# Reading the moving columns of every projection in two interleaved runs, with two moves in the first projection, in a four-layer transformer kernel

## The chip, the cores and the metric

One Trainium2 chip, one of its NeuronCores. The metric is device time in microseconds from the start to the end of one execution. TensorE (PE) multiplies, VectorE (DVE) and ScalarE (ACT) work on elements, GpSimd (POOL) on a few small rows, SyncE (SP) issues most of the DMAs.

## What is computed

Two small transformers of two layers each run one after the other on 256 tokens with 1024 features, all in float32. Layer by layer:

```python
x = x + fox_mixer(rms_norm(x, g))       # 16 heads, causal softmax with a forget gate
x = x + square(relu(rms_norm(x, g) @ w_up)) @ w_down
x = x + mla_mixer(rms_norm(x, g))       # 8 heads, low-rank q, shared low-rank k and v
x = x + square(relu(rms_norm(x, g) @ w_up)) @ w_down
x = rms_norm(x, g)
x = x + gla_mixer(rmsnorm(x, g))        # 4 heads, gated linear attention in chunks of 64
x = x + (silu(conv(h @ w_a)) * conv(h @ w_u)) @ w_down
x = x + (b * conv(c * u)) @ w_out       # b, c, u = rmsnorm(x, g) @ w_in
x = x + (silu(conv(h @ w_a)) * conv(h @ w_u)) @ w_down
return rmsnorm(x, g)
```

The work is nearly all in the projections `h @ w` with weights of 1024 rows and up to 5632 columns.

## The kernel before

**Split operands.** A float32 product is made of three matmuls of type fp32r. Each weight and each activation is kept as a high part and a low part: `wh` is the weight rounded to fp32r (a cast on ACT, line 294, or 291 with a gain), `wl` is the rest (a subtraction on DVE, line 312, or 308), and `hh` and `hl` are the same for the normalized activations. `mm3` issues `hh*wh`, `hh*wl` and `hl*wh` into one PSUM tile. Line 339 is the only line that issues these matmuls, so the profile gives them all under L339, told apart by their tiles: a name such as `up<-hh,wh` is the output tile, the moving operand and the stationary one.

**Two kinds of projection.** `proj`, `proj_wide` and `accum` keep 128 tokens stationary and move 512 (or 264, 320, 384) weight columns; their output has tokens on the partitions. `proj_T` keeps 128 weight columns stationary and moves the 256 tokens; its output is transposed, and two such outputs of 256 columns lie side by side in a PSUM tile of 512. Attention, the chunks of the linear attention and the transposes use plain float32 operands that are not split, with the same `mm` or with `transpose`.

**Evacuation.** When a PSUM tile is complete, a callback reads it: `by_row` on DVE (lines 399 and 401, times a row of scales), `add_x` on DVE (579 and 581, onto the residual), `scaled` on ACT (591, times a column of scales), a Relu on ACT (616), and a few more. `scaled_wide` cuts the two halves of a 528-column output into 512 columns of v and 16 of a gate.

**Weights.** SP loads raw weights into four buffers; `pump` casts the next units ahead (five buffers each of `wh` and `wl`), `pump_lo` makes their low parts.

**Order.** Most of the order comes from the program itself: `after(n, f)` runs `f` after `n` ticks, and a tick is one group of three matmuls (or six); the table `DLY` holds the delays. The engines run in program order, so what one waits for holds up all that comes behind it. The beginning, `start`, is written out by hand in a manual schedule: transposes of the four blocks of `x`, gains, the high and low parts of each block (`high(t, c)` and `low(t, c)` for token half t and feature half c), and the first weight splits between them. `norm` gathers the sums of squares; its last `stat` sets the scales on POOL and, where a row of them is wanted (`row`), calls `make_row` after `DLY[35]` ticks, which is 1: a DVE copy (line 144), two transposes on PE (line 502), an ACT copy (line 148). The row's readers are the `by_row` calls.

Of the kernel before, what the change touches and what calls it, by code (L numbers as in the profile page):

```python
# [15 lines left out]
ALU = mybir.AluOpType  # L16
# [144 lines left out]
class Builder:  # L161
# [178 lines left out]

    def mm3(self, ps, h, u, kk, n, start, stop):
# [18 lines left out]
    def proj(self, h, nk, n, evac, tiles=None, k0=0):  # L360
# [3 lines left out]
        while k < nk:  # L364
            u = self.unit()
            for kk in range(u.kn):
                for t in range(2):
                    self.mm3(ps[t][:, :n], h.get(t, k), u, kk, n, k == 0, k == nk - 1)
                    if k == nk - 1:
                        evac(t, ps[t])  # L370
                    self.tick()
                k += 1

    def proj_T(self, h, nk, evac, tile_fn=None):
# [4 lines left out]
        while k < nk:  # L379
            u = self.unit()  # L380
            for kk in range(u.kn):
                hh, hl = h.both(k)
                for f in range(4):
                    o = ps[f // 2][:, f % 2 * S:f % 2 * S + S]
                    wh, wl = [x[:, kk, f * P:(f + 1) * P] for x in (u.hi, u.lo)]
                    self.mm(o, wh, hh, k == 0 and f % 2 == 0, False)
                    self.mm(o, wl, hh, False, False)
                    self.mm(o, wh, hl, False, k == nk - 1)
                    if f % 2:
                        if k == nk - 1:  # L390
                            evac(f // 2, ps[f // 2])
# [3 lines left out]
    def by_row(self, out, ps, row, mul=None):  # L395

        r = lambda x: x.rearrange("p (i s) -> p i s", i=2)
        if mul is None:
            self.nc.vector.tensor_tensor(out=r(out), in0=r(ps), in1=row, op=ALU.mult)
        else:  # L400
            self.nc.vector.scalar_tensor_tensor(out=r(out), in0=r(ps), scalar=mul, in1=row, op0=ALU.mult, op1=ALU.mult)  # L401

    def proj_wide(self, h, evac, tile_fn):
# [3 lines left out]
        for k in range(8):  # L407
            if k % 2 == 0:
                u = self.unit()
            for t in range(2):  # L410
                hh, hl = h.get(t, k)
                for i in range(2):
                    o = ps[t][i][:, :n]
                    wh, wl = [x[:, k % 2, i * n:i * n + n] for x in (u.hi, u.lo)]
                    self.mm(o, hh, wh, k == 0, False)
                    self.mm(o, hh, wl, False, False)
                    self.mm(o, hl, wh, False, k == 7)
                if k == 7:
                    evac(t, *ps[t])
                self.tick()  # L420

    def scaled_wide(self, out, a, b, col):

        n = WIDE // 2
        self.scaled(out[:, 0:n], a[:, 0:n], col)
        self.scaled(out[:, n:512], b[:, 0:512 - n], col)
        return b[:, 512 - n:n]

    def accum(self, acc, h, ks, first, last, done=None, cs=(0, 1)):

        for c in cs:
            k = 0
            while k < len(ks):
                u = self.unit()
                for kk in range(u.kn):
                    for t in range(2):
                        self.mm3(acc[t][c], h.get(t, ks[k]), u, kk, 512, first and k == 0, last and k == len(ks) - 1)
                        if last and k == len(ks) - 1:
                            done(t, c, acc[t][c])
# [3 lines left out]
    def accum_by_token(self, acc, h, ks, done):  # L443
# [4 lines left out]
        self.nc.vector.tensor_tensor(out=xs, in0=acc[1][1], in1=xs, op=ALU.add)  # L448
        for t in range(2):
            for c in range(2):  # L450
                if not (t and c):
# [3 lines left out]
                    done(t, c, acc[t][c], 0)  # L455
                    continue
                for o in (0, 256):
                    ps = self.up_tile()[:, 0:256]
                    for i, k in enumerate(ks):
                        hh, hl = h.get(t, k)  # L460
                        wh, wl = [x[:, i, o:o + 256] for x in (us[c].hi, us[c].lo)]
                        self.mm(ps, hh, wh, i == 0, False)
                        self.mm(ps, hh, wl, False, False)
                        self.mm(ps, hl, wh, False, i == n - 1)
                        self.tick()
                    done(t, c, ps, o)
# [77 lines left out]
    def norm(self, gains, square=False, row=None, tile_fn=None, early=0):  # L544
# [7 lines left out]
        def stat(t, c):  # L552
            self.square_sum(ss[:, 2 * c + t:2 * c + t + 1], self.x[t][c], 512, 1.0 / 32.0)
            seen.append(1)
            if len(seen) == 4:
# [6 lines left out]
                if row is not None:  # L562
                    self.after(DLY[35], lambda: out.make_row(row))
# [9 lines left out]
    def add_x(self, hook, scale=None):  # L573
        nc = self.nc

        def done(t, c, ps, o=None):
            xs = self.x[t][c] if o is None else self.x[t][c][:, o:o + ps.shape[1]]
            if scale is None:
                nc.vector.tensor_tensor(out=xs, in0=ps, in1=xs, op=ALU.add)
            else:  # L580
                nc.vector.scalar_tensor_tensor(out=xs, in0=ps, scalar=scale[:, t:t + 1], in1=xs, op0=ALU.mult, op1=ALU.add)
# [7 lines left out]
    def scaled(self, out, ps, col):  # L589

        self.nc.scalar.activation(out=out, in_=ps, func=AF.Copy, scale=col)
# [15 lines left out]
    def ffn1(self, h, rs, hook):  # L607
# [360 lines left out]
    def mla(self, h, rs, hook):  # L968
# [21 lines left out]
        def ev_kv(t, ps):  # L990
            c = self.tmp_tile()
            self.scaled(c[:, :256], ps[:, :256], rs[:, t:t + 1])
            self.scaled(kc[:, t * 64:(t + 1) * 64], ps[:, 256:320], rs[:, t:t + 1])
# [28 lines left out]
        def ev_q(t, ps):  # L1022
            c = self.tmp_tile()
            self.scaled(c[:, :384], ps[:, :384], rs[:, t:t + 1])
# [101 lines left out]
    def gla(self, h, rs, hook):  # L1126
# [93 lines left out]
        def ev_g(i):  # L1220
            def f(t, ps):
                gs = self.tmp_tile()
                nc.scalar.activation(out=gs, in_=ps, func=AF.Silu, scale=rs[:, t:t + 1])
# [198 lines left out]
    def sc(self, h, rs, hook):  # L1422
# [9 lines left out]
        def ev_u(i):  # L1432
            def f(b, ps):
                z = cs.pop(b)
                nc.vector.tensor_tensor(out=z, in0=ps, in1=z, op=ALU.mult)
# [8 lines left out]
        def ev_b(i):  # L1444
            def f(b, ps):
                c = cv.pop(b)
                nc.vector.tensor_tensor(out=c, in0=ps, in1=c, op=ALU.mult)
# [280 lines left out]
```

## Time and profile before

| | before |
|---|---|
| median of 3 runs | 1157.27 us (1157.15 to 1157.37) |
| the profiled execution | 1156.24 us |
| its span | 1154.5 us |
| PE busy | 1142.0 us (99%) |
| PE weight loads busy (beside matmuls) | 1030.1 us (89%) |
| DVE busy | 804.8 us (70%) |
| ACT busy | 610.9 us (53%) |
| matmuls recorded | 7769 |
| DMA moved | 207.30 MB, mean 180 GB/s |

A matmul's own duration in the profile reaches from its start to its modelled end and overlaps the next one's; the time that a row of matmuls takes is their distance from start to start. The table gives averages over stages; the rows below give single stretches.

### The profile page before, as it was taken

Reading aid. Unit: us, or ns where it says so; the run is one execution under the profiler, and the core shown is the slowest. Engines: PE = TensorE matmul, PEld = TensorE weight load, DVE = VectorE, ACT = ScalarE, POOL = GpSimd, SP = SyncE. Lnnn points to the kernel's source line nnn. Section 1 sums busy time; section 2 is a strip of 40 time slices with the busy share of each in tenths; the row PEclk is TensorE's granted clock in tenths of the full one; section 3 lists DMA queues with packets and bytes.
Section 4 is the critical chain, followed back from the end, with each engine's and each line's share of the span. In section 5 each row is a group of like instructions: output and inputs, shape, how many; then the busy total and the mean of one; then the engine's idle time right before and its main releaser. Section 6 shows DMA issues by size and latency. Waiting matters only on the chain.

```text
span 1154.5 us, 19192 instructions
## 1 busy us (share of the span) xinstructions
PE 1142.0 (99%) x7769; PEld 1030.1 (89%) x7769; DVE 804.8 (70%) x1196; ACT 610.9 (53%) x923; POOL 33.2 (3%) x55
## 2 busy tenths in 40 slices
PE   8999999999999999999999999999999999999997
PEld 6987998998888999899898789999989999999996
DVE  6686755555686755555788569777786668887775
ACT  5465554445665545444563556455555446555453
POOL 0000100000000100000010000000001000000001
PEclk9999999999999999999999999999999999999999
DMA  9744455555463556555555355556665564656551
GB/s 341 276 146 146 160 197 191 183 183 167 135 203 120 168 192 195 192 184 183 185 178 170 110 165 164 180 179 191 200 217 185 194 185 134 196 175 213 183 159 62
DMA packets 137802, 207.30 MB, mean 180 GB/s; under 512 B 10529, under 2 KB 65009, under 8 KB 137713
## 3 DMA queue, kind: packets, MB, share of 16 engines
q1 hardware_dynamic: 136576, 203.89, 55.1%
q10 hardware_dynamic: 1136, 2.17, 0.5%
q8 instruction: 61, 1.00, 0.4%
q14 instruction: 29, 0.23, 0.1%
HBM read 204.97 MB, written 1.07 MB: 178 GB/s over the span
## 4 chain that ended last, share of the span: by engine, by line
PE 92%; DVE 5%; ACT 2%; issue 1%; POOL 0%; ACTq 0%; DVEq 0%; POOLq 0%
PE up L339 52%; PE acc L339 37%; DVE wl L312 1%; PE acc L502 1%; ACT p L672 1%; DVE p L691 1%; PE tp L502 1%; ACT wh L294 0%; DVE p L682 0%; ACT junk L535 0%; PE tp L512 0%; DVE kT L1207 0%; PE acc L1582 0%; DVE pT L700 0%; DVE bias L758 0%
## 5 line engine op out<-in xcount | busy, mean ns | idle before, releaser
L312 DVE TENSOR_TENSOR wl<-raw,wh 128x1024 fp32r<-128x1024 f32 (+2 forms) x373 | 454.1, 1219 | 261.4 <-ACT wh L294 259.5
L294 ACT CAST wh<-raw 128x1024 fp32r<-128x1024 f32 (+2 forms) x373 | 389.5, 1045 | 432.3 <-PE up L339 278.2
L339 PE MATMUL up<-hh,wh 128*128 128x256 f32 x1564 | 439.2, 281 | 0.0
L339 PE MATMUL up<-hh,wl 128*128 128x256 f32 x1564 | 437.7, 280 | 0.0
L339 PE MATMUL up<-hl,wh 128*128 128x256 f32 x1564 | 436.5, 280 | 0.0
L339 PEld LDWEIGHTS up<-hh,wh 128*128 128x128 f32 x1564 | 294.3, 188 | 3.0 <-issue 1.5
L339 PEld LDWEIGHTS up<-hh,wl 128*128 128x128 f32 x1564 | 294.1, 188 | 1.5
L339 PEld LDWEIGHTS up<-hl,wh 128*128 128x128 f32 x1564 | 294.2, 188 | 0.3 <-DVE hl L491 0.2
L339 PE MATMUL acc<-wh,hh 128*128 128x512 f32 (+1 forms) x606 | 235.8, 389 | 0.2 <-DVE mx L691 0.2
L339 PE MATMUL acc<-wh,hl 128*128 128x512 f32 (+1 forms) x606 | 233.3, 385 | 0.0
L339 PE MATMUL acc<-wl,hh 128*128 128x512 f32 (+1 forms) x606 | 232.8, 384 | 0.0
L339 PEld LDWEIGHTS acc<-wh,hl 128*128 128x128 f32 x606 | 113.8, 188 | 24.5 <-DVE hl L708 0.3
L339 PEld LDWEIGHTS acc<-wh,hh 128*128 128x128 f32 x606 | 113.8, 188 | 23.1 <-DVE mx L691 0.6
L339 PEld LDWEIGHTS acc<-wl,hh 128*128 128x128 f32 x606 | 113.9, 188 | 21.6
L1340 DVE SCALAR_TENSOR_TENSOR tmp<-tmp,vecs,tmp 128x255 f32<-128x255 f32 x192 | 78.0, 479 | 18.0 <-ACT tmp L1338 18.0
L339 PE MATMUL up<-wh,hh 128*128 128x512 f32 (+4 forms) x142 | 53.9, 382 | 0.3 <-DVE tmp L401 0.3
L339 PE MATMUL up<-wl,hh 128*128 128x512 f32 (+4 forms) x142 | 51.6, 364 | 1.3 <-DVE wl L312 1.3
L339 PE MATMUL up<-wh,hl 128*128 128x512 f32 (+4 forms) x142 | 51.4, 364 | 0.0
L1338 ACT ACTIVATE tmp<-tmp,vecs 128x256 f32<-128x256 f32 x96 | 40.9, 497 | 0.0
L1349 DVE TENSOR_TENSOR hl<-tmp,hh 128x512 fp32r<-128x512 f32 x58 | 38.2, 685 | 0.0
L1348 ACT CAST hh<-tmp 128x512 fp32r<-128x512 f32 x58 | 34.2, 622 | 2.2 <-DVE tmp L1393 2.2
L339 PEld LDWEIGHTS up<-wh,hh 128*128 128x128 f32 x142 | 26.7, 188 | 7.5 <-issue 3.4
(205 smaller groups left out, 770.5 us busy)
## 6 DMA issues: line engine op xcount, KB each, us to landing
raw<-ffn_w_up SPq DMA_DIRECT2D x176, 256.0 KB, 4.1
raw<-ffn_w_up SPq DMA_DIRECT2D x32, 1024.0 KB, 5.4
raw<-ffn_w_down SPq DMA_DIRECT2D x32, 1024.0 KB, 5.0
raw<-ffn_w_down SPq DMA_DIRECT2D x44, 512.0 KB, 6.5
raw<-sc_w_in SPq DMA_DIRECT2D x12, 1024.0 KB, 5.2
raw<-fox_w_in SPq DMA_DIRECT2D x10, 1024.0 KB, 9.4
raw<-gla_w_in SPq DMA_DIRECT2D x10, 1024.0 KB, 5.1
raw<-fox_w_out SPq DMA_DIRECT2D x4, 1024.0 KB, 5.0
```

Source lines behind the costliest of these rows:

```text
L294: self.last_hi = nc.scalar.copy(hi[:, :kn, :w], self.raws[r][:, k:k + kn])
L312: self.last_wl = nc.vector.tensor_tensor(out=u.lo[:, :kn, :w], in0=self.raws[r][:, k:k + kn], in1=u.hi[:, :kn, :w].bitcast(F32), op=ALU.su ...
L339: self.nc.tensor.matmul(out, lhsT, rhs, start=start, stop=stop, skip_group_check=True)
L502: self.nc.tensor.transpose(tp[:, i * P:(i + 1) * P], src[:, i * P:(i + 1) * P], self.ident)
L672: self.nc.scalar.activation(out=p[:, o:o + n], in_=p[:, o:o + n], func=AF.Exp, scale=scale, bias=nm[:, j:j + 1], accum_out=sm[:, j:j + 1])
L691: self.nc.vector.tensor_tensor_reduce(out=p[:, o:o + n], in0=lgs[h][:, w], in1=bias(h)[:, w], scale=1.0, scalar=NEG, op0=ALU.add, op1=ALU. ...
L1338: nc.scalar.activation(out=out, in_=z, func=AF.Copy, scale=w[:, 2:3])
L1340: nc.vector.scalar_tensor_tensor(out=out[:, d:], in0=z[:, :S - d], scalar=w[:, 2 - d:3 - d], in1=out[:, d:], op0=ALU.mult, op1=ALU.add)
L1348: nc.scalar.copy(hi, src)
L1349: nc.vector.tensor_tensor(out=lo, in0=src, in1=hi.bitcast(F32), op=ALU.subtract)
```

## The change

Every matmul of the split projections now goes through `mmw`. It hands the moving operand over as two runs, the first and the second half of its columns, taken in turn: column 0, column n/2, column 1, column n/2 + 1 and so on. The output is written in consecutive order, so PSUM holds the columns woven. Whoever reads PSUM undoes this by a view (`woven`) that takes every second column, and `like` gives the other operands the same shape. Where an instruction cannot take so many dimensions, it is cut in two (`by_row` with a factor, `scaled_wide`); the evacuation of the 320 columns of the shared k and v now copies all 320 in one piece, and the 64 rotary columns again.

In the first projection the low part of the second weight unit is made ahead of the last activation block's low part (`pump_lo(2)` before `low(1, 1)`), and the first layer's row of scales is made 12 ticks after the scales are set, not 1 (`row_at`). Other rows keep 1.

The diff, cut to its core:

```diff
+    def mmw(self, out, lhsT, rhs, start, stop):
+        self.mm(out.rearrange("p (b a) -> p b a", a=2), lhsT, rhs.rearrange("p (a b) -> p b a", a=2), start, stop)
+
+    @staticmethod
+    def woven(ps, n=1):
+        return ps.rearrange("p (b a) -> p a b", a=2) if n == 1 else ps.rearrange("p (i b a) -> p i a b", i=n, a=2)
...
     def mm3(self, ps, h, u, kk, n, start, stop):
         hh, hl = h
         wh, wl = u.hi[:, kk, :n], u.lo[:, kk, :n]
-        self.mm(ps, hh, wh, start, False)
-        self.mm(ps, hh, wl, False, False)
-        self.mm(ps, hl, wh, False, stop)
+        self.mmw(ps, hh, wh, start, False)
+        self.mmw(ps, hh, wl, False, False)
+        self.mmw(ps, hl, wh, False, stop)
...
     def by_row(self, out, ps, row, mul=None):
-        r = lambda x: x.rearrange("p (i s) -> p i s", i=2)
+        out, row = self.like(out, ps), self.like(row, ps)
         if mul is None:
-            self.nc.vector.tensor_tensor(out=r(out), in0=r(ps), in1=row, op=ALU.mult)
+            self.nc.vector.tensor_tensor(out=out, in0=ps, in1=row, op=ALU.mult)
         else:
-            self.nc.vector.scalar_tensor_tensor(out=r(out), in0=r(ps), scalar=mul, in1=row, op0=ALU.mult, op1=ALU.mult)
+            for i in range(2):
+                self.nc.vector.scalar_tensor_tensor(out=out[:, i], in0=ps[:, i], scalar=mul, in1=row[:, i], op0=ALU.mult, op1=ALU.mult)
...
     def scaled_wide(self, out, a, b, col):
         n = WIDE // 2
-        self.scaled(out[:, 0:n], a[:, 0:n], col)
-        self.scaled(out[:, n:512], b[:, 0:512 - n], col)
-        return b[:, 512 - n:n]
+        m = n // 2
+        self.scaled(out[:, 0:n], a, col)
+        self.scaled(out[:, n:n + m], b[:, 0], col)
+        self.scaled(out[:, n + m:512], b[:, 1, :m - 16], col)
+        return b[:, 1, m - 16:]
...
-                    self.after(DLY[35], lambda: out.make_row(row))
+                    self.after(row_at, lambda: out.make_row(row))
...
             def f(b, ps):
                 r = self.tmp_tile()
-                nc.scalar.activation(out=r, in_=ps, func=AF.Relu)
+                nc.scalar.activation(out=self.like(r, ps), in_=ps, func=AF.Relu)
...
             stat(1, 1)
             low(0, 1)
+            self.pump_lo(2)
             low(1, 1)
-            self.pump_lo(2)
...
-        hook, rs = self.norm([(h, self.vec("mix0"))], row=0)
+        hook, rs = self.norm([(h, self.vec("mix0"))], row=0, row_at=12)
```

The reading order itself does not show in a list of instructions, since a matmul's size stays the same. The two moves do. On DVE, in `start` and the beginning of the first layer (`hl_182` is the low part of the second feature half's activations, `wl_187` of the second weight unit, `rs_117` the scales; lines from 1543 on are 25 higher in the change):

```order
L1568 TENSOR_TENSOR hl_182<-tmp_174,hh_181 128x4x128
L1568 TENSOR_TENSOR hl_182<-tmp_184,hh_181 128x4x128
L312 TENSOR_TENSOR wl_187<-raw_106,wh_186 128x2x512
L312 TENSOR_TENSOR wl_229<-raw_106,wh_228 128x2x512
L144 COPY tmp_212<-rs_117 128x256
L312 TENSOR_TENSOR wl_240<-raw_231,wh_239 128x1056
L312 TENSOR_TENSOR wl_246<-raw_231,wh_245 128x1056
L312 TENSOR_TENSOR wl_250<-raw_234,wh_249 128x1056
```

and in the change:

```order
L1593 TENSOR_TENSOR hl_182<-tmp_174,hh_181 128x4x128
L312 TENSOR_TENSOR wl_187<-raw_106,wh_186 128x2x512
L1593 TENSOR_TENSOR hl_182<-tmp_184,hh_181 128x4x128
L312 TENSOR_TENSOR wl_222<-raw_106,wh_221 128x2x512
L312 TENSOR_TENSOR wl_233<-raw_224,wh_232 128x1056
L312 TENSOR_TENSOR wl_239<-raw_224,wh_238 128x1056
L312 TENSOR_TENSOR wl_243<-raw_227,wh_242 128x1056
L144 COPY tmp_280<-rs_117 128x256
```

The second weight unit's low part has moved ahead of the second `hl_182`, and the copy of the scales behind three splits of the wide projection. On PE, the matmuls that read them (the transposes of line 502 are 21 lines further down in the change), before:

```order
L339 MATMUL up_119<-wh_186,hh_181 128x512
L339 MATMUL up_118<-wl_187,hh_181 128x512
L339 MATMUL up_118<-wh_186,hl_182 128x512
L339 MATMUL up_119<-wl_187,hh_181 128x512
L339 MATMUL up_119<-wh_186,hl_182 128x512
L339 MATMUL up_118<-wh_186,hh_181 128x512
L339 MATMUL up_118<-wl_187,hh_181 128x512
L502 MATMUL tp_214<-ident,tmp_212 128x128 x2
L339 MATMUL up_118<-wh_186,hl_182 128x512
```

and, where the two transposes now stand:

```order
L339 MATMUL acc_299<-wh_232,hh_147 128x264
L339 MATMUL acc_299<-wl_233,hh_147 128x264
L523 MATMUL tp_282<-ident,tmp_280 128x128 x2
L339 MATMUL acc_299<-wh_232,hl_148 128x264
L339 MATMUL acc_296<-wh_232,hh_147 128x264
```

They have moved past the rest of the first projection, 16 matmuls, and the first 11 of the wide one.

## Rows read from the trace of the kernel before

**Rows 1.** The page, busy us, share of the span and instructions of each engine

```profile
PE   1142.0 (99%) x7769; PEld 1030.1 (89%) x7769; DVE 804.8 (70%) x1196; ACT 610.9 (53%) x923; POOL 33.2 (3%) x55
```

**Rows 2.** The page, chain that ended last: share of the span by engine, by line

```profile
PE 92%; DVE 5%; ACT 2%; issue 1%; POOL 0%; ACTq 0%; DVEq 0%; POOLq 0%
PE up L339 52%; PE acc L339 37%; DVE wl L312 1%; PE acc L502 1%; ACT p L672 1%; DVE p L691 1%; PE tp L502 1%; ACT wh L294 0%; DVE p L682 0%; ACT junk L535 0%; PE tp L512 0%; DVE kT L1207 0%; PE acc L1582 0%; DVE pT L700 0%; DVE bias L758 0%
```

**Rows 3.** The chain in order of time: start us, us, what, merged matmuls

```profile
24.37 9.98 PE acc L339 x82
...
147.58 11.09 PE acc L339 x48
158.66 11.22 PE up L339 x96
...
248.01 11.35 PE up L339 x96
...
721.90 11.28 PE up L339 x96
```

**Rows 4.** Timeline of PE, linear attention: start us, us, what, merged

```profile
634.85 1.89 PE L339 MATMUL acc<-v,both 128*128 128x256 f32 x8
```

**Rows 5.** PE's groups by shape: line, what, count, busy us, mean ns, idle

```profile
L339 PE MATMUL up<-hh,wh 128*128 128x256 f32 x1564 | 439.2, 281 | 0.0
...
L339 PE MATMUL acc<-wh,hh 128*128 128x512 f32 x558 | 222.1, 398 | 0.2 <-DVE mx L691 0.2
...
L339 PE MATMUL up<-wh,hh 128*128 128x512 f32 x90 | 37.4, 419 | 0.3 <-DVE tmp L401 0.3
...
L339 PE MATMUL acc<-wh,hh 128*128 128x264 f32 x48 | 13.7, 286 | 0.0
...
L339 PE MATMUL acc<-hh,wh 128*128 128x256 f32 x44 | 12.3, 280 | 0.0
...
L339 PE MATMUL up<-wh,hh 128*128 128x264 f32 x16 | 4.6, 290 | 0.0
...
L339 PE MATMUL acc<-v,both 128*128 128x256 f32 x16 | 3.8, 379 | 0.0
```

**Rows 6.** Timeline of PE, first projection: start us, us, what, idle before

```profile
13.03 0.63 PE L339 MATMUL up<-wh,hh 128*128 128x512 f32 x2
14.96 0.50 PE L339 MATMUL up<-wl,hh 128*128 128x512 f32 x1 [1.31 <-DVE wl L312]
...
17.56 0.44 PE L502 MATMUL tp<-ident,tmp 128*128 128x128 f32 x2 [0.94 <-DVE tmp L144]
```

**Rows 7.** Timeline of DVE and of ACT in the same stretch

```profile
13.08 0.69 DVE L1568 TENSOR_TENSOR hl<-tmp,hh 128x512 fp32r<-128x512 f32 x1 [0.78 <-ACT hh L1564]
13.69 2.35 DVE L312 TENSOR_TENSOR wl<-raw,wh 128x1024 fp32r<-128x1024 f32 x2
17.21 0.29 DVE L144 COPY tmp<-rs 128x256 f32<-128x256 f32 x1 [1.17 <-POOL rs L542]
17.42 4.76 DVE L312 TENSOR_TENSOR wl<-raw,wh 128x1056 fp32r<-128x1056 f32 x4
...
11.48 1.04 ACT L294 CAST wh<-raw 128x1024 fp32r<-128x1024 f32 x1
```

**Rows 8.** Stretches: length, busy us of PE, PEld, DVE, ACT, POOL, clock, DMA

```profile
53.00:97.00 44.00, 43.80 (x367) 35.43 (x366) 38.47 (x135) 26.75 (x76) 0.18 (x1) 1.00 0.53 184
...
125.00:300.00 175.00, 175.00 (x1139) 159.08 (x1138) 100.70 (x105) 85.16 (x105) 3.63 (x4) 1.00 0.55 180
...
593.00:619.00 26.00, 26.00 (x209) 25.20 (x207) 25.40 (x37) 16.66 (x21) 0.00 (x0) 1.00 0.49 160
...
676.00:863.00 187.00, 187.00 (x1339) 175.36 (x1338) 147.65 (x212) 104.23 (x146) 2.75 (x3) 1.00 0.59 183
```

**Rows 9.** Line 399's instructions: count, ns min/median/max, first and last start us

```profile
L399 DVE TENSOR_TENSOR tmp<-up,rowb x48: 680/684/692, 693.4 to 1129.9; 128x512 f32<-128x512 f32 x48
L399 DVE TENSOR_TENSOR kT<-up,rowb x8: 662/681/684, 46.9 to 346.4; 128x512 f32<-128x512 f32 x8
```

More of the change, by code (lines that the diff above doesn't have):

```diff
@@ L447, in accum_by_token @@
         xs = self.x[1][1]
-        self.nc.vector.tensor_tensor(out=xs, in0=acc[1][1], in1=xs, op=ALU.add)
+        ps = self.woven(acc[1][1])
+        self.nc.vector.tensor_tensor(out=self.like(xs, ps), in0=ps, in1=self.like(xs, ps), op=ALU.add)
         for t in range(2):
@@ L542, in rsqrt, with norm @@
         nc.gpsimd.tensor_tensor(out=out, in0=out, in1=self.mhalf[:, :n], op=ALU.pow)
-    def norm(self, gains, square=False, row=None, tile_fn=None, early=0):
+    def norm(self, gains, square=False, row=None, tile_fn=None, early=0, row_at=1):
         ss = self.small.tile([P, 4], F32, tag="ss", name=self.name("ss"))
@@ L576, in done @@
         def done(t, c, ps, o=None):
-            xs = self.x[t][c] if o is None else self.x[t][c][:, o:o + ps.shape[1]]
+            xs = self.x[t][c] if o is None else self.x[t][c][:, o:o + ps.shape[1] * ps.shape[2]]
+            x3 = self.like(xs, ps)
             if scale is None:
-                nc.vector.tensor_tensor(out=xs, in0=ps, in1=xs, op=ALU.add)
+                nc.vector.tensor_tensor(out=x3, in0=ps, in1=x3, op=ALU.add)
             else:
-                nc.vector.scalar_tensor_tensor(out=xs, in0=ps, scalar=scale[:, t:t + 1], in1=xs, op0=ALU.mult, op1=ALU.add)
+                nc.vector.scalar_tensor_tensor(out=x3, in0=ps, scalar=scale[:, t:t + 1], in1=x3, op0=ALU.mult, op1=ALU.add)
             if o is None:
@@ L589, in scaled @@
     def scaled(self, out, ps, col):
+        if len(ps.shape) > 2:
+            out = self.like(out, ps)
         self.nc.scalar.activation(out=out, in_=ps, func=AF.Copy, scale=col)
@@ L1222, in f @@
                 gs = self.tmp_tile()
-                nc.scalar.activation(out=gs, in_=ps, func=AF.Silu, scale=rs[:, t:t + 1])
+                nc.scalar.activation(out=self.like(gs, ps), in_=ps, func=AF.Silu, scale=rs[:, t:t + 1])
                 def gain():
@@ L1434, in f @@
                 z = cs.pop(b)
-                nc.vector.tensor_tensor(out=z, in0=ps, in1=z, op=ALU.mult)
+                nc.vector.tensor_tensor(out=self.like(z, ps), in0=ps, in1=self.like(z, ps), op=ALU.mult)
                 def go():
@@ L1446, in f @@
                 c = cv.pop(b)
-                nc.vector.tensor_tensor(out=c, in0=ps, in1=c, op=ALU.mult)
+                nc.vector.tensor_tensor(out=self.like(c, ps), in0=ps, in1=self.like(c, ps), op=ALU.mult)
                 self.after(DLY[29], lambda: self.split_pair(c, y, 4 * i + 2 * b))
```

43 lines of the change are left out of this document (24 added, 19 removed).

## The prediction

> **What bounds the kernel now.** I read the page first. TensorE (PE) is busy for 1142.0 of 1154.5 us, VectorE (DVE) for 70% of the span [rows 1], and the granted clock is 1.00 in the stretches that I looked at, the 2.4 GHz level [rows 8]. The chain of waits agrees: 92% of the end is set by PE, and 52% and 37% by the two kinds of matmul that line 339 issues [rows 2]. None of the lines that empty PSUM (399, 401, 579, 581, 591, 616) is among those that the chain names. So the time is the number of matmuls times their pitch (start to start), and the next question is what the pitch is made of.
>
> The chain in order of time gives pitches, since it merges a run of back-to-back matmuls into one piece [rows 3]: 48 matmuls with 512 moving columns in 11.09 us are 231.0 ns each; 96 with 256 columns take 11.22 to 11.35 us, 116.9 to 118.2 ns, and I use 117.3; 82 with 264 columns take 9.98 us, 121.7 ns. At one column a cycle of 2.4 GHz, 512 columns need 213.3 ns and 256 need 106.7. So 17.7 ns and 10.6 ns are lost, and the loss grows with the columns.
>
> Is that loss in the engine or in the supply of columns? The kernel holds a control. Its attention matmuls are plain fp32, not split: 8 of them with 256 columns take 1.89 us [rows 4], of which the last one's own 0.379 [rows 5] is not pitch, so (1.89 - 0.379) / 7 = 215.9 ns. That is two cycles a column (213.3 ns) and 2.5 ns more. A stream that asks for a column every second cycle loses only a fixed 2.5 ns; one that asks every cycle loses four to seven times as much. Contention with other engines does not look like the cause: the 256-column pitch is 11.22 to 11.35 us for 96 where DVE is busy for 100.7 of 175 us, and 11.28 [rows 3] where it is busy for 147.7 of 187 us [rows 8]. What is left is the way in which one run of consecutive fp32 columns is fetched, and that is what the change alters.
>
> **The change, part by part.** *The reading order.* The counts are in rows 5: (1564 + 44) x 3 = 4824 matmuls with 256 columns, (558 + 90) x 3 = 1944 with 512, (48 + 16) x 3 = 192 with 264. (The few with 320 and 384 columns I leave out.) They write PSUM in consecutive order as before, and no matmul is added. No row of the trace shows a moving operand read in two interleaved runs, so its price has to be bounded. The lower end: one cycle a column and the fixed 2.5 ns of the plain matmuls, which gives 109.2, 215.8 and 112.5 ns. The upper end: two cycles a column, as the plain ones, 215.9, 429.2 and 222.5 ns. I take the lower end: two streams half a tile apart give each stream the two cycles a column at which the plain matmuls show no loss, so the row nearest to what each stream now asks is the plain one, halved. The sum is 4824 x 8.1 ns = 39.1 us, 1944 x 15.2 ns = 29.5 us, 192 x 9.2 ns = 1.8 us: 70.4 us.
>
> The row speaks for this, a rule speaks against it. The Trainium skill (Advanced Engine Details and Errata, section Memory Cachelines) says that SBUF has 16-byte lines and that at least two hits in a row on one line are needed to absorb its latency; here neighbours lie 512 bytes or more apart, so no two reads in a row would meet one line. By that rule the order would be slower, not faster; no run here shows it yet. By the rows the sum is near 1091 us, by the rule it is that of the second rival below.
>
> *Where the gain does not arrive.* In two stages the chain runs through DVE and ACT rather than PE: 53 to 97 us (DVE busy for 38.5 of 44) and 593 to 619 us (25.4 of 26) [rows 8]. A faster PE waits there. At the average rate, 70.4 / 1142 = 6.2%, these 70 us would have given 4.3 us; I take off all of it, and 66.1 us stay. Elsewhere DVE has room: in 676 to 863 us it is busy for 147.7 us and PE would still need some 175.
>
> *The evacuations.* PSUM columns now lie woven, so DVE and ACT read every second one. No row shows a strided read. The lower bound is nothing: a read of 512 columns from PSUM takes 684 ns [rows 9], and one from SBUF 0.69 us [rows 7], so these reads are paced by the element. The upper bound is a doubling; since no such line reaches the list of the chain, whose last entries round to 0% (under 0.5%, 5.8 us) [rows 2], I put it at 6 us. I take 2 us, nearer to the rows. The split calls (two halves where a scalar factor is used, two pieces where the wide projection's tail is cut off) are eight or so more instructions on DVE and ACT, hidden beside PE; without that cover each would cost a few tenths of a microsecond.
>
> *The weight split ahead of the low part.* PE waits 1.31 us at 14.96 us for the low part of a weight [rows 6], which DVE makes at 13.69 us behind an hl that itself waited for ACT [rows 7]. Its input, the cast that starts at 11.48 and takes 1.04 us, is there at 12.52 [rows 7]. Placed ahead, the split runs from 12.52 to 13.74 us, and PE is ready at 13.03 + 2 x 0.231 = 13.49, so 0.25 us of the wait stay. What is late next is that hl: 13.74 + 0.69 = 14.43 us; its first reader is the fourth matmul from 13.8 us, at about 14.5, so it fits.
>
> *The row of scales later.* PE stood for 0.94 us at 17.56 us for the DVE copy of line 144 [rows 6], which waited for POOL and began at 17.21 [rows 7], with all later matmuls behind it. Eleven ticks later PE comes to it near 20 us; on DVE the copy now stands behind three more wide splits of about 1.2 us each (4.76 us for four in the trace), so it ends near 20 us too. I count 0.2 us of a new wait there. The two starts together give 1.31 + 0.94 - 0.25 - 0.2 = 1.8 us. The row's first user, the first key projection's evacuation, is at 46.9 us [rows 9]. On ACT's queue the small load of fox_b_f now comes behind two evacuations; its reader stands behind the whole wide projection, so nothing waits for it. SP's and POOL's queues keep their order.
>
> *Sum.* The profiled execution took 1156.24 us. 1156.2 - 66.1 - 1.8 + 2.0 = 1090.3. It ran 1.0 us under the median of the runs shown (1157.27), so the forecast is 1091 us.
>
> **The rivals.**
> (1) Half the loss stays. If the order hides only a part of what a fetch costs, say half, 35.2 - 2.2 = 33 us are gained: 1156.2 - 33 - 1.8 + 2 + 1 = 1124 us. For it: the loss per matmul is 10.6 ns at 256 columns and not half of 17.7, so not all of it goes with the columns.
> (2) Slower: two cycles a column. If each of the alternating reads pays a fetch of its own, SBUF delivers a column every second cycle, as it does for the plain matmuls. The place is every matmul of rows 5; the price 4824 x 98.6 + 1944 x 198.2 + 192 x 100.8 ns = 475.6 + 385.3 + 19.4 = 880 us, all on PE, which has no idle time to hide it: 1156.2 + 880 - 1.8 + 2 + 1 = 2037 us. It decides early: the start's gain and the evacuations about cancel (1.8 against 2.0 us), so a woven pitch that is 0.3 ns longer for 256 columns is enough (2.3 us over 4824 + 2 x 1944 such pieces). Against it: the plain matmuls' half rate belongs to another kind of matmul and need not come from its reads. For it: nothing in the trace ever read alternately.
> (3) The order changes nothing: the loss belongs to each column wherever it comes from. Then only the start and the evacuations remain, 1156.2 - 1.8 + 0 to 2 + 1 = 1155 to 1157 us, no change that can be told. Against it: the plain matmuls use the same path without the loss.
>
> **How the numbers follow.** The forecast's own case 0.60, rival 1 0.15, rival 2 0.17, rival 3 0.08. The forecast's own range is 1083 us (nothing lost in the two stages, both waits gone, no price for the evacuations) to 1100 us (6 us for them, and new waits behind DVE). To leave out no more than 2 in 10, the range reaches to rivals 1 and 3: 1083 to 1158 us; left out is rival 2 and a little below. About 0.2%, 2.3 us, is what a measurement of this kernel can tell from no change. Faster by more than that: the forecast, rival 1 and a quarter of rival 3, 0.77; within it 0.06; slower 0.17.
>
> **What would show it.** In the chain of the changed kernel 48 matmuls with 512 columns should take 10.4 us and 96 with 256 columns 10.5 us; the plain attention matmuls should stay at 1.89 us for 8. The PE waits at 14.96 and 17.56 us should shrink to a few tenths, line 144's copy should begin near 20 us, and the evacuations of 512 columns should stay near 684 ns. The prediction is wrong if the 512-column pitch stays at 231 ns (rival 3), is near 223 (rival 1) or near 429 (rival 2), or if the pitch falls and the span does not: then DVE's share, above all from 676 to 863 us, should be near 100%.

## The result, and the profile after

The changed kernel takes 1104.32 us (median of 4 runs, 1103.79 to 1104.49) against 1157.24 us (4 runs, 1157.15 to 1157.37) for the kernel before: a ratio of 0.9542, 95% interval 0.9525 to 0.9558. That is 52.9 us less; the forecast was 66.3 us less, 1091 us. The direction held, and most of the gain came from the pitch, as forecast; 13 us of it did not come, and the time lies above the forecast's own range (1083 to 1100 us).

The page of the changed kernel, the parts on busy time and on the chain that ended last:

```profile
PE 1087.3 (99%) x7769; PEld 1003.4 (91%) x7769; DVE 801.4 (73%) x1200; ACT 609.2 (55%) x927; POOL 30.4 (3%) x55
...
PE 87%; DVE 7%; ACT 2%; DMA 1%; issue 1%; SPq 0%; ACTq 0%; DVEq 0%
```

Against [rows 1, 2]: PE's share of the chain fell from 92% to 87%, DVE's rose from 5% to 7%, and 1% is now a transfer of weights at the start. Its order in time (start us, length us, engine, tile, line, count):

```profile
9.49 9.44 DMA raw<-fox_w_in
...
24.77 7.88 PE acc L339 x70
...
50.77 1.05 ACT wh L294
...
142.62 10.36 PE acc L339 x48
152.98 10.72 PE up L339 x96
```

These answer to [rows 3]. 48 matmuls with 512 columns take 10.36 us, 215.8 ns each, as forecast to the tenth. 70 with 264 columns take 7.88 us, 112.6 ns (forecast 112.5). But 96 with 256 columns take 10.72 us, **111.7 ns and not 109.2**, and they do so in every piece of the chain. The granted clock was 1.00 in the stretches read of both kernels.

PE's timeline at the start (start us, length us, line, what, idle before):

```profile
7.39 3.51 PE L339 MATMUL up<-raw,tmp 128*128 128x512 f32 x6 [0.25 <-DMA raw<-fox_w_in]
...
11.52 0.46 PE L339 MATMUL up<-wh,hh 128*128 128x512 f32 x1
...
14.97 0.48 PE L339 MATMUL up<-wl,hh 128*128 128x512 f32 x1 [0.18 <-DVE wl L312]
...
21.66 0.44 PE L523 MATMUL tp<-ident,tmp 128*128 128x128 f32 x2 [0.44 <-DVE tmp L144]
```

The waits of 1.31 and 0.94 us [rows 6] are 0.18 and 0.44 us. What the forecast had left out is in the first row: the plain fp32 matmuls of the first projection (four calls in two passes, eight records) now read woven too, and stand 540 ns apart, where they stood 429 ns apart before.

The evacuations, two lines of DVE (count, ns min/median/max, first and last start us, shape):

```profile
L416 DVE TENSOR_TENSOR tmp<-up,rowb x48: 681/684/691, 664.1 to 1079.1; 128x512 f32<-128x512 f32 x48
...
L419 DVE SCALAR_TENSOR_TENSOR qT<-up,rowb x4: 413/416/417, 57.7 to 59.9; 128x256 f32<-128x256 f32 x4
```

A woven read of 512 PSUM columns takes 684 ns, exactly as the straight one did [rows 9]. The split calls cost 416 ns for a half, but two of them overlap to 0.75 us against 0.68 us for the whole.

**Where the gain arrived.** From the starts of the same split matmuls in both traces, beside what the measured pitches alone should give:

| stretch before, us | gained, us | by the pitches, us |
|---|---|---|
| 53 to 97 | 0.35 | 1.62 |
| 125 to 300 | 9.90 | 9.87 |
| 300 to 386 | 2.41 | 3.90 |
| 405 to 566 | 9.22 | 9.20 |
| 566 to 619 | 0.57 | 2.99 |
| 690 to 851 | 8.29 | 8.54 |
| 851 to 968 | 4.84 | 6.07 |
| 968 to 1146 | 9.59 | 9.60 |
| all from 34 us on | 50.3 | 58.1 |

Where PE alone sets the chain, the pitch is the whole story. In four stretches (53 to 97, 300 to 386, 566 to 619 and 851 to 968 us) it is not. In the last of them, too, the chain of the changed kernel passes through DVE; its longest such piece is

```profile
814.80 3.25 DVE tmp L1365 x8
```

### The profile page after: what moved, and what is told of

It is laid out like the page before. It is cut to its first block, busy times and chain, and to the rows that moved or that the text cites. A ratio compares the mean times of both kernels' runs of the same rounds, so it can differ in the third digit from the quotient of the medians.

```text
span 1102.7 us, 19201 instructions
## 1 busy us (share of the span) xinstructions
PE 1087.3 (99%) x7769; PEld 1003.4 (91%) x7769; DVE 801.4 (73%) x1200; ACT 609.2 (55%) x927; POOL 30.4 (3%) x55
## 4 chain that ended last, share of the span: by engine, by line
PE 87%; DVE 7%; ACT 2%; DMA 1%; issue 1%; SPq 0%; ACTq 0%; DVEq 0%
PE up L339 52%; PE acc L339 33%; DVE wl L312 2%; DMA raw<-fox_w_in 1%; ACT wh L294 1%; PE acc L523 1%; PE tp L523 1%; ACT p L697 1%; DVE p L716 1%; DVE x L602 0%; DVE p L707 0%; PE tp L533 0%; DVE tmp L1365 0%; DVE pT L725 0%; DVE kT L1232 0%
## 5 line engine op out<-in xcount | busy, mean ns | idle before, releaser
L339 PE MATMUL up<-hh,wh 128*128 128x256 f32 x1564 | 431.7, 276 | 0.0
L339 PE MATMUL up<-hh,wl 128*128 128x256 f32 x1564 | 430.1, 275 | 0.0
L339 PE MATMUL up<-hl,wh 128*128 128x256 f32 x1564 | 429.4, 275 | 0.0
L339 PEld LDWEIGHTS up<-hh,wh 128*128 128x128 f32 x1564 | 300.1, 192 | 2.9 <-issue 1.5
L339 PEld LDWEIGHTS up<-hh,wl 128*128 128x128 f32 x1564 | 300.1, 192 | 0.9
L339 PEld LDWEIGHTS up<-hl,wh 128*128 128x128 f32 x1564 | 299.8, 192 | 0.3 <-DVE hl L512 0.2
L339 PE MATMUL acc<-wh,hh 128*128 128x512 f32 (+1 forms) x606 | 227.4, 375 | 0.2 <-DVE mx L716 0.2
L339 PE MATMUL acc<-wh,hl 128*128 128x512 f32 (+1 forms) x606 | 225.1, 371 | 0.1
L339 PE MATMUL acc<-wl,hh 128*128 128x512 f32 (+1 forms) x606 | 224.8, 371 | 0.0
```

The lines of the kernel that those rows point to most:

```text
L339: self.nc.tensor.matmul(out, lhsT, rhs, start=start, stop=stop, skip_group_check=True)
```

## The experiments

Twelve kernels ran. Two questions lead: why the woven order helps at all, and why 256 columns stop at 111.7 ns and some stages keep their length.

### The reading order by itself

A kernel of matmuls alone, 48 of each kind, with the moving operand (split fp32 unless said) read in different orders. The orders are views of the operand:

```python
woven(n):   src.rearrange("p (a b) -> p b a", a=2)
chunk(n,c): src.rearrange("p (a b c) -> p b a c", a=2, c=c)
near(n,r):  src.rearrange("p (g a r) -> p g r a", a=2, r=r)
step(n,s):  src.rearrange("p (b s) -> p b s", s=s)[:, :, i % 2]
```

> Leaves out the whole network (the output is zeros): 48 back-to-back matmuls for each of 29 ways of reading the moving columns, fp32r unless said. Straight 512 and 256 should give 231 and 117 ns, woven 216 and 111.6. THEORY LOAD (the 256-column pitch is now set by the weight load of 128 columns): woven 240, 192 and 128 columns stay near 111.6 ns, 264 gives 112.5 and 320 135.8; with 64 stationary columns 256 woven columns fall to 109.2; alternating 512 and 256 columns gives 325.1 ns a pair. THEORY SHORT RUNS (runs of 128 columns are read slower than runs of 256): 240, 192 and 128 columns go on falling (105, 85 and 58 ns), 64 stationary columns change nothing, and the alternating pair takes 327.5. On the order: THEORY LINE (what is lost is lost at a change of line, and any second run hides it): taking 2, 4 or 16 columns from each half in turn also gives 216, and four runs too. THEORY NEIGHBOUR (two neighbouring reads in a row cost): only column-by-column alternation cures, 4 and 16 at a time are back near 231, while halves only 8 to 64 columns apart do cure. By the rule on 16-byte lines in the Trainium skill, steps of 4 and 8 columns (16 and 32 bytes) would lose much, up to 429 ns, and the woven order too.

PE's timeline of it (one row is 48 matmuls of a kind; B, D, H, P, S stand for 2, 4, 8, 16, 64 columns, shift A for one column, fourA for four runs in turn; C, H and I of the woven rows are 256, 192 and 128 columns, M is 256 with 64 stationary ones):

```profile
24.70 11.04 PE L44 MATMUL straightA<-mv,st 128*128 128x512 f32 x48
35.59 10.52 PE L44 MATMUL wovenA<-mv,st 128*128 128x512 f32 x48
45.95 11.53 PE L44 MATMUL shiftA<-mv,st 128*128 128x512 f32 x48
57.31 16.48 PE L44 MATMUL chunkB<-mv,st 128*128 128x512 f32 x48
73.61 12.18 PE L44 MATMUL chunkD<-mv,st 128*128 128x512 f32 x48
85.63 11.69 PE L44 MATMUL chunkP<-mv,st 128*128 128x512 f32 x48
...
108.08 11.04 PE L44 MATMUL nearB<-mv,st 128*128 128x512 f32 x48
118.96 10.52 PE L44 MATMUL nearD<-mv,st 128*128 128x512 f32 x48
...
160.40 13.75 PE L44 MATMUL fourA<-mv,st 128*128 128x512 f32 x48
173.98 21.82 PE L44 MATMUL stepB<-mv,st 128*128 128x512 f32 x48
...
254.59 5.52 PE L44 MATMUL wovenC<-mv,st 128*128 128x256 f32 x48
...
277.22 5.50 PE L44 MATMUL wovenH<-mv,st 128*128 128x192 f32 x48
282.56 5.50 PE L44 MATMUL wovenI<-mv,st 128*128 128x128 f32 x48
...
293.26 5.40 PE L44 MATMUL wovenM<-mv,st 128*64 128x256 f32 x48
```

The pitch is the distance of two starts by 48, or, free of the change from one kind to the next, the mean inside a kind. Straight 512 columns: 226.7 ns. Woven halves: (45.95 - 35.59) / 48 = 215.8. Two columns from each half in turn: 340. Runs that alternate at a distance of 2 columns: 226.7; of 4, 8, 16 and 64 columns: 215.8. Every second column: 451. So the loss is in the order of the reads, and two runs four columns apart cure it as well as two halves do. Not every second run does: 4 and 16 columns from each half in turn take 250 and 240 ns, and four runs 283. LINE had expected 216 for all of these; NEIGHBOUR, with 231 for the first two, was nearer. One difference stays open: straight 512 columns take 226.7 ns here and 231.0 in the kernel, while woven ones take 215.8 in both.

The last four rows settle the 256 columns. Woven 256, 240, 192 and 128 columns take 111.1 to 111.7 ns with 128 stationary columns; with 64 stationary columns the 256 fall to 109.2. **The load of 128 stationary columns is a floor of 111.7 ns**, whatever streams past it. That it is the load is inferred from this fall; the load's own records, which overlap the matmuls, are 192 ns long for 128 columns and 136 ns for 64. (The Trainium skill, TensorE: Matmul & The Clock Gate, section LDWEIGHTS (loading the stationary operand), gives P / 1.2 ns for P stationary columns, by which an estimate for 128 is 107 ns; the measured floor is 5 ns above it.) Kinds that alternate, 512 and 256 columns in turn, took 327.6 ns a pair, the sum of both pitches: a short one is not helped by a long neighbour, which the load theory had expected (325.1 ns).

### Which operand's order pays

The changed kernel with the 256-column kind (tokens moving, line 403 on) read straight again:

```diff
-                    self.mmw(o, wh, hh, k == 0 and f % 2 == 0, False)
+                    self.mm(o, wh, hh, k == 0 and f % 2 == 0, False)
```

(so too for its two other products, and the evacuation takes the straight view).

> The change, but where the 256 tokens are the moving columns they are read straight. If the two kinds add up, the gain of the 256-column matmuls, 4824 x 5.7 ns = 27.5 us, is lost again: 1131 us. RIVAL, part of it had no room to arrive because DVE and ACT hold the 256-column stages: less than 22 us, under 1126 us.

1127.98 us (ratio 0.9751, interval 0.9736 to 0.9766). Its chain:

```profile
144.15 10.36 PE acc L339 x48
154.51 11.19 PE up L339 x96
...
176.06 11.26 PE up L339 x96
```

512 columns keep 215.8 ns, 256 go back to 116.6 to 117.3. So weaving the 256-column kind is worth 1127.98 - 1104.32 = 23.7 us, between the two expectations; by the forecast's 8.1 ns it would have been 39.1.

### The two moves at the start, alone and left out

The change without them (the weight split stays behind the low part, the row of scales at its old place), and the kernel before with them alone.

> The change with its two moves at the start undone. If the two moves pay as I forecast (1.8 us), this is 1106 us. RIVAL, the first weights come from DMA so late that waits only change their names: 1104 us, no difference from the change that can be told.

> The kernel before with only the two moves at the start. If they pay as forecast, 1155.4 us. RIVAL (the DMA of the first projection sets this stretch): 1157 us, within 0.2% of before.

Without them 1106.20 us (1105.77 to 1106.37; 1.9 us above the change); alone 1155.04 us against 1156.86 us (ratio 0.9985, interval 0.9976 to 0.9994), 1.8 us. The forecast's term for them was 1.8 us.

### Odd distances, plain fp32 and bf16

A second kernel of matmuls alone.

> A kernel of matmuls alone, 48 to a pattern, operands in SBUF; its output is zeros, so nothing of the reference is computed. Split fp32 first: straight 512 columns 226.7 ns and woven halves 215.8 ns, as in the first pattern run. If a column costs extra only where its neighbour before lies on the same 16-byte line (theory LINE), a half distance of 255, 254 or 252 columns reads like 256, that is 215.0, 214.2 and 212.5 ns for 510, 508 and 504 columns; alternating runs of two columns (which has a same-line neighbour in every pair) lie between 216 and 227; a straight read shifted by 4 or 16 columns stays at 226.7, by 2 columns it is slower. If it is the distance that must be a round number of bytes (theory BANK), the odd distances fall back to 227 or more. Plain fp32, 512 columns: straight in and out 429 ns, woven in and straight out 540 ns (the start of the changed kernel shows both). Theory READ: the weave in the moving operand alone costs the plain matmul 111 ns, so woven in with PSUM written back in natural order is 540 too, and straight in with PSUM written woven is 429. Theory WRITE: the order of the PSUM write counts, then the last is near 540 and the one before differs from it. bf16: 215.8 for all three.

```profile
136.92 41.36 PE L46 MATMUL plainS<-raw 128*128 128x512 f32 x96
178.12 52.00 PE L46 MATMUL plainW<-raw 128*128 128x512 f32 x96
229.95 52.00 PE L46 MATMUL plainN<-raw 128*128 128x512 f32 x96
281.79 41.36 PE L46 MATMUL plainT<-raw 128*128 128x512 f32 x96
322.99 10.52 PE L48 MATMUL bfS<-mb 128*128 128x512 bf16 x48
333.35 23.41 PE L48 MATMUL bfW<-mb 128*128 128x512 bf16 x48
```

A plain fp32 matmul shows as two records, one for each pass; the times are for one record. S is straight, W woven in, N woven in and written back in natural order, T straight in and written woven: 429, 540, 540, 429 ns. READ holds: the order of the PSUM write costs nothing, the woven read costs 111 ns. Half distances of 255, 254 and 252 columns gave 215.0, 214.2 and 212.5 ns, so BANK falls. Two misses: two columns from each half in turn took 340 ns again (expected 216 to 227), which speaks against LINE as worded, and straight reads shifted by 4 and 16 columns took 231.6 and 229.0 ns, not 226.7. And bf16, expected at 215.8 in every order, took **484.5 ns woven**: the order that cures split fp32 halves the rate of bf16.

### Two streams

One theory fits most of the surprises: a split fp32 operand is read as two streams, of the even and of the odd places in the order of reading, and each wants several reads in a row from one 16-byte line. Woven halves give each stream four, straight reading two, every second column one. A third kernel of matmuls alone sets it against the theory that only neighbours matter.

> Matmuls alone, 48 to a pattern, 512 columns; the output is zeros. Theory STREAMS: a split fp32 operand is read as two streams, one of the even and one of the odd columns, and each stream wants its reads to follow one another on a 16-byte line; bf16 and plain fp32 are one stream. Then reads per line and stream set the pitch. Split fp32: woven (4 in a row) 215.8 ns; straight (2) 226.7; every second column read straight (1) 451; halves of every second column woven (2) 227 to 240, although neighbours lie on different lines; halves of every fourth column woven (1) 450 or so. Alternating runs at a distance of 2 columns 226.7, of 4 columns 215.8. Plain fp32: straight (4) and alternating at distance 2 (same line) 429; alternating at distance 4 (1) 540; every second column (2) 429; every fourth (1) 540. bf16: straight and alternating at distance 4 columns (8 bytes, same line) 215.8; at distance 8 (1) 484; every second (4) and every fourth (2) 216 to 230, every eighth (1) 450 to 484. Rival NEIGHBOUR: two successive columns on one line cost time, two on different lines do not; then halves of every second and of every fourth column woven read at 215.8, every second column straight should have been slow for its pairs only, and bf16 has no reason to differ. 256 columns woven: the load of the weights sets the floor, 111.7 ns with 128 stationary columns; by the load's length (one column a cycle and some 58 ns) 96 and 64 stationary columns fall to the 109.2 ns of the columns themselves.

Its timeline, cut at the kinds (the x50 rows hold a neighbour or two of the kinds beside them):

```profile
45.61 11.08 PE L44 MATMUL wovstep<-mv,st 128*128 128x512 f32 x48
...
56.07 22.37 PE L44 MATMUL wovstep<-mv,st 128*128 128x512 f32 x50
...
78.26 21.94 PE L44 MATMUL step<-mv,st 128*128 128x512 f32 x48
...
122.17 11.10 PE L44 MATMUL near<-mv,st 128*128 128x512 f32 x48
```

Split fp32: woven halves of every second column 227.2 ns, of every fourth 453.2; every second column straight 453.3; alternating at distance 2 and 4 columns 227.1 and 215.8. All as STREAMS said, and NEIGHBOUR (215.8 for the first two) falls. Alternating runs in plain fp32 (429.2 on one line, 543.3 on two) and bf16 (215.8 and 485.5) followed it as well. Its counts failed for steps outside split fp32: plain fp32 took 450 and 900 ns for every second and fourth column (expected 429 and 540), bf16 451 for every fourth (expected at most 230) and 900 for every eighth (expected 450 to 484).

Nor do they give every row of split fp32. Two columns from each half in turn, and four runs, leave each stream one read in a row and should take 450 ns; they took 340 and 283. With 4 and 16 columns in turn there are two, and they took 250 and 240, not 227. So the count puts the split fp32 rows in order (four reads in a row 215.8 ns, two 226.7 to 250, one 283 to 461) and is shown for the orders of this third kernel, but it does not set the pitch by itself. What else does, and how the engine reads the other types, stays open. 256 columns took 111.7 ns with 128 stationary columns and 109.2 with 96 and, at full clock, with 64, as the load floor asks.

The Trainium skill's rule (Advanced Engine Details and Errata, section Memory Cachelines), that at least two hits in a row on a 16-byte line are needed, agrees with the order of these rows if hits are counted in each stream: one costs most, 283 to 461 ns, though two still cost more than four. Counted over neighbouring columns, as for the prediction's second rival, it is refuted by 215.8 ns.

### The plain matmuls, and the row of scales later still

The changed kernel ran again, and then with the plain matmuls read straight:

```diff
-            self.mmw(ps[t], hg[t, 0][:, k * P:(k + 1) * P], self.raws[0][:, k], k == 0, False)
+            self.mm(ps[t].rearrange("p (b a) -> p a b", a=2), hg[t, 0][:, k * P:(k + 1) * P],
+                    self.raws[0][:, k].rearrange("p (a b) -> p a b", a=2), k == 0, False)
```

> The changed kernel once more, as the base for the other two runs of this call: 1104.3 us by its first measurement, plain fp32 matmuls at the start 540 ns apart.

> The changed kernel, but the eight plain fp32 matmuls at the start read their moving operand straight and write PSUM woven. Theory READ: they return from 540 to 429 ns each, the first split matmul starts up to 0.9 us earlier, and the time falls by 0.3 to 0.9 us (the rest is taken by waits for the transfer of the next weights, which the chain of the changed kernel names at the start). Rival WRITE: the pitch stays at 540 ns and the time within 0.2 us.

1104.44 us (1104.19 to 1104.60) and 1104.32 us (1104.22 to 1104.52). The first split matmul comes 0.5 us earlier (10.8 against 11.3 us), but the cast of the next weights starts where it did (18.9 and 18.8 us), the wait for the row of scales behind it grows from 0.5 to 0.7 us, and the rest of the start ends where it did. In the chain of the changed kernel this cast follows the landing of the weights (9.49 + 9.44 = 18.93 us). The gain is hidden; the rival's "within 0.2 us" came true for another reason than its own. Then the row one place later (`row_at=13`), on top of this:

> The changed kernel with the eight plain matmuls at the start read straight (as in the run before this) and the row of scales put one matmul group later still. If PE's last wait at the start (0.4 to 0.7 us for the DVE copy of that row, which stands behind a weight split on DVE) comes from where the row is put, it goes, and the time is 0.3 to 0.7 us below 1104.3. Rival: the row's readers or the transfer of the weights that the next matmuls need are late by as much, and the time stays within 0.2 us.

1104.29 us (1104.08 to 1104.38), no change. PE's waits (what it waited for: us, times, longest):

```profile
PE tp L523 <- DVE tmp L144: 1.0, 1, 1.0
```

The copy only stands behind one more weight split on DVE, and the wait grows to 1.0 us. The rival was right, by its second reason: the chain of this run leads from the landing of the weights at 18.7 us through their cast and two splits on DVE to the copy. The transfer and DVE's queue set the time here, not the place in PE's order.

### The stages that kept their length

In the changed kernel, PE's two slow stages by windows, as in [rows 8] (length; busy us of PE, PEld, DVE, ACT, POOL; clock, DMA share, GB/s):

```profile
50.80:93.60 42.80, 41.67 (x363) 34.05 (x361) 38.08 (x134) 25.83 (x73) 0.00 (x0) 1.00 0.53 185
566.60:593.00 26.40, 24.65 (x208) 23.96 (x206) 26.02 (x39) 17.14 (x21) 0.00 (x0) 1.00 0.51 173
```

DVE is full in the second, and the chain there is one of DVE pieces with weight splits (wl, line 312) as links:

```profile
584.05 1.12 DVE wl L312
585.16 1.14 DVE kT L1215
586.30 1.20 DVE kT L1232 x2
...
589.85 2.27 DVE wl L312 x2
592.12 0.68 DVE tmp L419 x2
```

First try: 18 splits go to POOL, which is idle.

```diff
-                self.last_wl = nc.vector.tensor_tensor(
+                j = self.n_wl
+                self.n_wl += 1
+                eng = nc.gpsimd if 16 <= j <= 24 or 188 <= j <= 196 else nc.vector
+                self.last_wl = eng.tensor_tensor(
```

> The changed kernel, but 18 of the 376 weight splits (the low parts, about 1.15 us each on DVE), nine in each of the two stages in which the chain runs through DVE and ACT, are made by POOL, which has almost nothing to do there. Theory CHAIN: DVE sets these two stages, which gained 0.3 and -0.2 us where the pitches give 1.6 and 1.3; with the splits off DVE the stages become 1 to 1.5 us shorter each, at the end 1101.5 to 1103 us against 1104.3, and PE's pitch sets them. Rival PORT: POOL's reads and writes slow DVE down, the DVE operations beside them take longer than before (over 1.3 times), and the time stays or grows, to 1108 us. Rival FLOOR: PE was filling the stages after all; DVE's idle time grows by 10 us and the time stays within 0.5 us.

1113.69 us (1112.26 to 1116.74), 9 us slower: PORT, and beyond its 1108 us. DVE's groups in 50 to 97 us (line, what, count, busy us, mean ns, idle), first of this run, then of the changed kernel:

```profile
L712 DVE TENSOR_SCALAR p<-p,rc 128x128 f32<-128x128 f32 x12 | 7.4, 618 | 0.2
L788 DVE TENSOR_TENSOR bias<-bias,csts 128x1024 f32<-128x1024 f32 x3 | 6.3, 2115 | 1.0 <-DMA bias<-rows 1.0
```

```profile
L707 DVE TENSOR_SCALAR p<-p,rc 128x128 f32<-128x128 f32 x14 | 4.1, 295 | 0.1
L783 DVE TENSOR_TENSOR bias<-bias,csts 128x1024 f32<-128x1024 f32 x3 | 3.7, 1221 | 0.0
```

The same DVE operations take 2.1 and 1.7 times as long beside POOL's splits of 2.5 us each. Not all of the 9 us are theirs alone. By the starts of the same matmuls 4.1 us were lost in the first stage and 4.0 us between 520 and 566 us. In the first stage (columns as above)

```profile
50.80:93.60 42.80, 39.82 (x338) 33.42 (x337) 36.11 (x108) 23.66 (x67) 21.72 (x9) 0.96 0.47 163
...
67.00 5.84 PE up L344 x36
```

PE waited, busy for 2.73 of the 4.30 us up to 67.0 us, and then ran at a granted clock of 0.50, the 1.2 GHz level, until 70.4 us: the 36 matmuls of the second row, a piece of the chain, took 1.8 us longer than at 111.7 ns.

Second try: the 18 splits are left out, and those units use `u.lo = u.hi`.

> The changed kernel, in which 18 of the 376 low parts of the weights are not made: nine units in each of the two stages where the chain runs through DVE and ACT (50.8 to 93.6 us and 566.6 to 593 us) use their high part in its place, so this part of the computation is left out, while TensorE issues the same matmuls. It takes 18 x 1.14 = 20 us off DVE and puts nothing on POOL, whose splits slowed DVE's other work down in the run before. Theory CHAIN: DVE's splits are a link of the chain in these stages (15% of it), and each stage becomes shorter until PE's own pitches set it, 1.2 to 1.5 us each: 1101.3 to 1102.3 us. Rival FLOOR: PE filled the stages already; 1104 us, and only DVE's idle time grows.

1103.07 us (1102.77 to 1103.56), above CHAIN's range. The first stage became 2.05 us shorter. The second did not: its nine units had been counted without 16 splits of line 308, and lay at 520 to 550 us in both tries. Leaving them out there was followed by a wait of 1.4 us for DVE. With the right nine (`205 <= j <= 213`):

> The run before with the second nine units where they were meant to be. There, the first nine lay in the first stage, which became 2.05 us shorter with a chain of PE alone, while the second nine had been counted off by the 16 splits of another line and lay at 520 to 545 us, where leaving them out cost 0.9 us by a later wait for DVE; the second stage kept its chain through DVE and its length. Now they lie from 566 to 593 us; as before, these units use their high part in place of the low part, so this part of the computation is left out. Theory CHAIN: the first stage is again 2 us shorter, the second 1 to 1.5 us, the 0.9 us are not lost, and the time is 1100.5 to 1101.5 us. Rival for the second stage: its chain goes on through the other DVE operations (the kT and LB lines), and only some tenths are gained there, 1101.8 to 1102.5 us.

1099.50 us (1099.28 to 1100.19; ratio 0.9504, interval 0.9491 to 0.9517), 1 us below CHAIN's range. The chain in the second stage, and windows over both (columns as above):

```profile
566.48 10.72 PE acc L346 x96
577.20 14.77 PE up L346 x127
```

```profile
51.00:92.00 41.00, 41.00 (x362) 33.89 (x361) 30.41 (x133) 27.09 (x79) 0.42 (x1) 1.00 0.56 197
563.00:589.00 26.00, 26.00 (x215) 25.44 (x214) 19.37 (x34) 17.39 (x22) 0.00 (x0) 1.00 0.61 203
```

The first stage is 2.05 us shorter, 566 to 619 us 2.3 us, and the chain in them is PE's alone. CHAIN holds: DVE, with the weight splits in its queue, set these stages (the loss there was 3.7 us of the gain; freed of the splits they give 4.4). Since this version leaves out part of the computation, it is no kernel to keep; none of the complete variants beat the change by more than the runs can tell.

## Why the prediction was right, and where it was not

**What bounds the kernel, and the control.** Right. The loss was in the supply of columns: the order of reading alone, with no matmul less, took 512 columns from 231.0 to 215.8 ns. Taking the plain matmuls' 2.5 ns as the floor gave the 512- and 264-column kinds to the tenth. (The 8 matmuls of that control are rows of the profile; a plain fp32 matmul shows as two, so the 2.5 ns are those of one pass.) The reason behind it, that two runs give each stream two cycles a column, was not borne out: the rows go with two streams, but by how many reads in a row each makes on one line. That the plain row carried over was in part luck, since the same order slows a plain fp32 matmul down.

**The sum over the matmuls: the step that failed.** "The lower end: one cycle a column and the fixed 2.5 ns ..., which gives 109.2". For 256 columns that lower end could not be reached, since the load of the weights holds the pitch at 111.7 ns. 4824 x 2.5 ns = 12.1 us of the 70.4 us were never there, nearly the whole miss. The plain control could not show it: at 215.9 ns its load had time to spare. The 320- and 384-column kinds, left out, gave 1.1 us back (48 matmuls each, from 146.4 to 135.8 and from 174.7 to 162.5 ns).

**Where the gain does not arrive.** The mechanism is shown for two stages; the term, 4.3 us, should have been 7.8 us (58.1 - 50.3). The two named stages lost 1.3 us (53 to 97) and 1.5 us (593 to 619). Taken as free were 566 to 593 us, where the same DVE chain begins (1.0 us), 300 to 386 us (1.5 us) and 851 to 968 us (1.2 us), both not tried by themselves, and tenths in most of the others. So the stages were charged too much and the rest nothing.

**The evacuations.** Sized at 2 us, measured at nothing: 684 ns on DVE before and after, and 599 and 598 ns for ACT's Relu. The row that compared PSUM with SBUF had pointed there.

**The start.** 1.8 us forecast, 1.8 us (alone) and 1.9 us (left out) measured; the row of scales cost 0.44 us of wait rather than 0.2. The plain matmuls, which the diff also weaves, were not costed: 8 x 0.111 = 0.9 us on PE, of which next to nothing reaches the end, since the weights that land at 18.9 us set what follows.

**The account.** 12.1 - 1.1 + (7.8 - 4.3) - 2.0 = 12.5 of the 13.3 us between forecast and result; the other 0.8 us have no place of their own.

**The rivals.** Half the loss staying (1124 us) and no change fell with the 512-column pitch; of the 256-column kind's 10.6 ns, though, nearly half did stay (111.7 against 106.7), from the load of the weights. The slow case (2037 us) did not happen, but for other operands the order is slower: the plain matmuls paid 540 for 429 ns, and bf16 484.5 for 215.8. It was the operand's type that decided, and the trace of before could not tell which type would pay.

## What to carry to other kernels

When a pitch is compared with its floor, look for every floor: the columns that stream, and the weights that must be loaded meanwhile, which with 128 stationary columns hold a matmul of 128 to 256 columns at 111 to 112 ns. Of the three types tried the woven order pays for split fp32 alone: it is worth 5 to 7% of a 512-column matmul there, while the same order adds a quarter to a plain fp32 matmul and more than doubles a bf16 one. And a gain per instruction is collected only in stages where that engine sets the chain; for each other stage, name the engine that will, and subtract.

## What the runs showed of the hardware

- Split fp32 operands: the pitch of 512 columns is ordered by the reads in a row that the even and the odd places of the reading order each make on 16 bytes: four 215.8 ns, two 226.7 to 250, one 283 to 461. Where the runs start matters a little too: straight reads shifted by 1, 2, 4 and 16 columns took 236.7, 233.3, 231.6 and 229.0 ns.
- Woven columns in PSUM cost neither the writing matmul (429 ns either way, plain fp32) nor DVE's read (684 ns either way).
- POOL's splits stretched DVE operations beside them from 295 to 618 ns and from 1221 to 2115 ns.
- In the third kernel of matmuls alone the granted clock was 0.50, the 1.2 GHz level, from 488.6 to 529.5 us. It fell while PE was busy without a gap (4.00 of the 4.00 us from 484 to 488 us) with bf16 matmuls that read every eighth column; these stood 900 ns apart before the fall and after it, so this pitch did not go by the clock. The next kind did: woven 256 columns with 64 stationary ones stood 212 ns apart until the clock rose and 109 ns after it.
- In the stretches read, the kernel before and the change show 1.00; with POOL's splits the clock was 0.50 from 67.0 to 70.4 us, after PE had stood waiting.
